# Long expert lists in a branch with two arms, a router that reads x itself, and later head norms

## The chip, the cores and the metric

One core of a Trainium2 chip. The metric is device time of one execution in microseconds (us), as the median of three runs. TensorE (PE) multiplies; its weight loads are listed apart as PEld. VectorE (DVE) and ScalarE (ACT) do elementwise work and empty the accumulators in PSUM, GpSimd (POOL) helps and issues some transfers, and SyncE (SP) issues most of them.

## The reference, cut to what matters

256 tokens of width 1024 in float32 pass four layers: two of a first block, two of a second. A layer of the first block is a token mixer and a mixture of 16 experts:

```
h = rmsnorm(x, norm2_g) * (1 + sc2) + sh2
scores = sigmoid(h @ w_router)              # 16 experts in 4 groups of 4
# best group by the sum of its two best (score + bias); its two best experts;
# their scores, normed to sum 1, are the weights in combine
for e in range(16):
    he = silu(h @ w_gate[e]) * (h @ w_up[e])      # 1024 -> 512
    y += combine[:, e] * (he @ w_down[e])         # 512 -> 1024
x = x + g2 * y
```

Each token so goes to 2 of 16 experts, and how many tokens an expert gets depends on the data. The second block begins with an attention in which 16 query heads and 4 key heads of width 64 are normed per head (rmsnorm over 64), turned by position, and scored against 256 own and 256 context keys, in a window and with a sink.

## The kernel before, in words

Everything is kept as xT: features on partitions (8 chunks of 128, KD), 256 tokens along the row. Wide products are done as three products of rounded operands: a weight is split into a high part (ScalarE, L513) and the rest (VectorE or POOL, L514), an activation likewise, and mm3 (L532 to L534) multiplies high by high, high by low and low by high. Products of plain float32 operands are two instructions each in the trace.

The program is written as straight Python, unrolled. A scheduler orders each engine's instructions by its own estimate of when they are ready, with program order as priority. An If is a unit for it: nothing moves over its borders, each engine takes the branch for itself, and a shorter path adds to the semaphores what the longer one would have.

**Token mixer, end (L986 to L993).** A loop of four turns multiplies by w_out, adds the result to two chunks of xT (L990) and squares them; when all eight are summed, rnorm, the reciprocal root of the mean square of each token, is made by Ln and Exp (L399, L400).

**Router (L1059 to L1129).** hf = norm of xT with gain and shift (eight VectorE or POOL products, eight ScalarE passes), the router's product with hf in four column groups of the array (L1067), a copy, two transposes and a sum into tokens by experts (L1075), the clamp (L1076), the sigmoid as Exp, Ln, Exp, and some 20 small VectorE steps to combine weights (cmb), and to each token's place in its experts' lists (pos). Beside it hf is turned into rows per token (L1137) and split into ht, high and low (L440, L441).

**Experts (L1340 to L1376).** A list has 64 places (SL). places makes a 0/1 table of tokens by places for four experts (PG), features multiplies ht by it, which gathers the tokens' columns (xg), in four steps of two chunks, each emptied by one copy (evac, VectorE and ScalarE in turn). For each expert e: gate_up, 64 places against 512 columns of gate and up (L1179, L1180); swiglu (Silu on ScalarE, product on VectorE); place(e - 2), which scatters expert e-2's weighted result into yT with its table PT (L1258); down of expert e-1 (L1224, L1225), whose result ScalarE and VectorE weight and split into y (L1228, L1229); turn, four transposes of the hidden row and a VectorE copy into he (L1203, L1204). After every even expert scatter_tab makes PT and the weights of two experts. After the third and fourth of a group of four, half of the next group's features. Last comes an If (L1373): a list longer than 64 runs beyond, which gathers the rest of the list, and does gate, up, down and scatter for up to 32 more places by themselves; a nested If (L1308) goes on with longer lists still.

**Weights.** An expert has six transfers of 1 MB. ahead(6e + 14) asks at expert e for what fills the queue to two experts ahead, on SP and POOL in turn; each waits for its buffer.

**Window attention (L1522 on).** For keys of context and own tokens, then for four groups of query heads: projection, head_norm (copy with gain, square, product with a swapping table, product that sums squares, turn by position, root, product), then copies into high and low parts. Then 16 units score (L1580 high key part over 128 rows, L1581 low key part over the 64 rows of the head's high query part), take softmax and multiply with values.

Of the kernel before, what the change touches and what calls it, by code (L numbers as in the profile page):

```python
# [18 lines left out]
T = 256  # L19
# [89 lines left out]
def tile_kernel(ctx, tc, A, out, dbg=None, stop=None):  # L109
# [97 lines left out]
    wrt = ctile([128, KD, 2 * NE], name="wrt")  # L207
    wnorm = ctile([128, 2], name="wnorm")

    def later_rows():  # L210
        nc.sync.dma_start(rbias, A["router_bias"][None, :].to_broadcast([128, NE]))
        nc.sync.dma_start(sink, A["win_sink_2"].to_broadcast([128, 16]))
        for j in range(2):
            nc.sync.dma_start(wrt[:, :, NE * j:NE * j + NE], A["w_router"].rearrange("(k p) e -> p k e", p=128))
# [350 lines left out]
    def token_mix(l):  # L565
        key = (0, l)
        with ExitStack() as es:
# [418 lines left out]
            st = Stats(P, lambda: sp.tile([128, T], F32, name=nm("sq"), tag="sq"))  # L986
            for n in range(4):
                ps = dense2(P, split_w(load_w(A["w_out"][l], 0, 8, 256 * n, 256), hlp, 8), mga, 8)
                for e in range(2):
                    V.scalar_tensor_tensor(xT[:, 2 * n + e], ps[:, e], mod(key, 2, 2 * n + e), xT[:, 2 * n + e], op0=OP.mult, op1=OP.add)  # L990
                    st.add(2 * n + e)
                ada(f"o{n}")
        dump(f"x_tm{l}", xT)  # L993
# [48 lines left out]
    def moe(l, experts):  # L1042
        key = (0, l)
        with ExitStack() as es:
# [14 lines left out]
            hf = mp.tile([128, KD, T], F32, name="hf", tag="b8", bufs=2)  # L1059
            gn = gain(key, 4, "norm2_g", 8 * l, f"gn2_{l}")  # L1060
            norm_split(xT, gn, lambda k: mod(key, 3, k), P, sp, [hf[:, k] for k in range(KD)], r=rnorm)
            dump(f"hf{l}", hf)

            lgp = ps_("gu")
            for k in range(KD):
                g = k % 4
                PE.matmul(lgp[32 * g:32 * g + 32, 0:T], wrt[:, k], hf[:, k], start=(k < 4), stop=(k >= 4), skip_group_check=True)  # L1067
            lgs = sp.tile([128, 512], F32, name=nm("lgs"), tag="gx", bufs=1)[:, 0:T]
            S.copy(lgs, lgp[:, 0:T])
            lgt = ps_("t")  # L1070
            for t in range(2):
                PE.transpose(lgt[:, 128 * t:128 * t + 128], lgs[:, 128 * t:128 * t + 128], ident)
            rt = mp.tile([128, 4, 2, NE], F32, name="rt")
            sc_, bi, cmb, pos = (rt[:, i] for i in range(4))
            V.tensor_reduce(sc_, lgt[:, 0:T].rearrange("p (t g e) -> p t e g", t=2, g=4)[:, :, 0:NE], axis=AX.X, op=OP.add)  # L1075
# [57 lines left out]
            for t in range(2):  # L1133
                for g in range(2):
                    ps = ps_("gu")
                    for k in range(4):
                        PE.transpose(ps[:, 128 * k:128 * k + 128], hf[:, 4 * g + k, 128 * t:128 * t + 128], ident)  # L1137
                    sl = slice(512 * g, 512 * g + 512)
                    split_act(ht[0][:, t, sl], ht[1][:, t, sl], ps)

            tc.keep_in_program_order(S.preload_act_table_set("silu_and_others"))

            def gather(dst, cols_, ks):

                for k0 in ks:
# [6 lines left out]
                    evac(dst[:, k0:k0 + 2], ps.rearrange("p (k n) -> p k n", n=T))  # L1152

            def scatter_tab(pg, es_, wc, tabs, tag="t"):

                m = len(es_)
                n = m * SL
                pw = sp.tile([128, 2, 2 * SL], F32, name=nm("pw"), tag="pw", bufs=1)
                ps = ps_(tag)
                for t in range(2):  # L1160
                    V.tensor_tensor(pw[:, t, :n].rearrange("p (e s) -> p e s", e=m), pg(t).bitcast(F32).rearrange("p (e s) -> p e s", e=m),
                                    cmb[:, t, es_[0]:es_[0] + m, None].to_broadcast([128, m, SL]), OP.mult)
                    PE.transpose(ps[:n, 128 * t:128 * t + 128], pw[:, t, :n], ident)
                j = sp.tile([128, T], BF, name=nm("jk"), tag="jk", bufs=1)
                S.activation(j[:n], ps[:n, :T], AF.Copy, accum_out=wc[:n])
                for i, (pt, w) in enumerate(tabs):
                    for r in (0, 64):
                        V.tensor_scalar(pt[r:r + 64], ps[SL * i:SL * i + SL, :T], 0.0, None, op0=OP.is_gt)
                        V.tensor_copy(w[r:r + 64], wc[SL * i:SL * i + SL])
# [49 lines left out]

            def down(he, e, w, y, tag):  # L1220

                py = ps_(tag)
                for j in range(4):
                    PE.matmul(py[0:64], he[:, j], cut(e, j, 0), start=(j == 0), stop=(j == 3), skip_group_check=True)  # L1224
                    m = PE.matmul(py[64:128], he[:, j], cut(e, j, 1), start=(j == 0), stop=(j == 3), skip_group_check=True)  # L1225
                    if j == 1:
                        yield m.ins
                S.activation(y[0], py, AF.Copy, scale=w)  # L1228
                V.scalar_tensor_tensor(y[1], py, w, y[0].bitcast(F32), op0=OP.mult, op1=OP.subtract)  # L1229
                yield m.ins  # L1230
# [29 lines left out]
            def beyond(e, w, level):  # L1260
# [12 lines left out]
                for h in range(2):  # L1273
                    ps = ps_("y" if h else "gu")
# [10 lines left out]
                evac(xo.rearrange("p (h j) s -> p j h s", h=2), ps.rearrange("p (j h s) -> p j h s", j=4, h=2))  # L1285
                ptl = sp.tile([128, T], F32R, name=nm("pto"), tag="pto", bufs=1)
                wc = sp.tile([128, 2], F32, name=nm("wc"), tag="wc", bufs=1)
                scatter_tab(lambda t: pg[:, t, 0:SL], [e], wc[:, 0:1], [(ptl, wc[:, 1:2])])
# [10 lines left out]
                y = [sp.tile([128, 512], F32R, name=nm("yo"), tag=f"yo{i}", bufs=1) for i in range(2)]  # L1299
# [5 lines left out]
                yield m  # L1305
# [6 lines left out]
            he_ = mp.tile([128, 4, SL], F32, name="he")  # L1312
# [28 lines left out]
            for e in range(NE):  # L1341
# [16 lines left out]
                place(e - 2)  # L1358
                if e:
                    for _ in down(he_, e - 1, tabs[e - 1][1], y_, "y"):  # L1360
                        pass
                turn(x_, he_)
                if e % 2 == 0:
                    for i in (e, e + 1):
                        tabs[i] = (mp.tile([128, T], F32R, name=nm("PT"), tag="PT", bufs=3),
                                   sp.tile([128, 1], F32, name=nm("w2"), tag="w2", bufs=3))
                    wc = sp.tile([128, 1], F32, name=nm("wp"), tag="wp")
                    scatter_tab(lambda t: lists[g][:, t, SL * j:SL * j + 2 * SL], [e, e + 1], wc, [tabs[e], tabs[e + 1]], "gu")
# [17 lines left out]
            if l:  # L1386
                mark = sp.tile([128, 1], F32, name=nm("mark"), tag="wp")
                with tc.issue_after(S.copy(mark, he_[:, 0, 0:1]).ins):
# [8 lines left out]
            for h in range(2):  # L1397
                fs = slice(256 * h, 256 * h + 256)
                py = ps_("t" if h else "y")[:, 0:256]
                for j in range(4):  # L1400
                    for q in range(2):
                        PE.matmul(py[64 * q:64 * q + 64], he_[:, j], cut(NE - 1, j, h)[:, 256 * q:256 * q + 256], start=(j == 0), stop=(j == 3),
# [25 lines left out]
    def win_attention(l, key):  # L1428
        with ExitStack() as es:
# [95 lines left out]
            def head_norm(ps, gcol, turn):  # L1525
# [4 lines left out]
                S.activation(s_, ps, AF.Square)  # L1530
                if turn:
# [11 lines left out]
                return x  # L1543


            for c, (a, th, tl) in ((1, (hc, ch, cl)), (0, (h, hh, hl))):
                ps = dense2(P, wk, a, 8)
# [263 lines left out]
```

## Time and profile before

| | |
|---|---|
| median of three runs | 1977.56 us (1974.22 to 1979.89) |
| the profiled execution | 1981.36 us, of which the profile's span is 1979.5 |
| instructions | 30922 |
| mean granted TensorE clock | 0.951 |
| data moved | 467.37 MB, 236 GB/s over the span |
| expert stages | 340.67 to some 640 us, and 949.93 to some 1240 us |

A stretch's busy time is the union of an engine's instructions in it. PEclk is the clock that the chip granted TensorE: 1.00 is 2.4 GHz, 0.50 is 1.2 GHz, a value in between a mean. An idle time in brackets stands ahead of an instruction, with what released it; a q behind an engine's name is its sequencer. 35 passes through swiglu in the trace are 32 experts and 3 long lists.

### The profile page before, as it was taken

What the parts mean: (1) busy time and instruction counts of PE and PEld (TensorE: products, weight loads), DVE (VectorE), ACT (ScalarE), POOL (GpSimd) and SP (SyncE); (2) the same over time, 40 slices, a digit from 0 to 9 for tenths busy, and PEclk for the clock granted to TensorE, in tenths of its full rate; (3) what the DMA queues carried; (4) which work ended last, traced back from release to release, by engine and by line L of the source; (5) the groups of instructions that cost most, each with busy time, mean ns of one, the idle gap of its engine ahead of it and who ended that gap; (6) DMA issues with size and microseconds to landing.
All of it is one profiled execution on the core that took longest, in us unless ns stands there. A gap on an engine that the chain in (4) does not pass through costs nothing. (4 is left out here: it accounts for less than half of the span.)

```text
span 1979.5 us, 30922 instructions
## 1 busy us (share of the span) xinstructions
PE 1779.8 (90%) x12451; PEld 1329.2 (67%) x12451; DVE 1034.1 (52%) x1893; ACT 885.6 (45%) x1492; POOL 323.1 (16%) x244
## 2 busy tenths in 40 slices
PE   6989998887888899998888977789899998989997
PEld 4767796334343777787434433666789997979997
DVE  5766454222122886555222222686466776677775
ACT  4544543111112544454111112886567675457874
POOL 2310241111111320233011110230200002430000
PEclk9999998998899899998899988899999999999998
DMA  9767784894896466896599955330386734576430
GB/s 324 256 231 293 275 285 188 339 384 174 300 412 241 170 220 239 297 337 222 224 403 407 391 219 193 118 128 1 124 300 236 264 130 171 181 259 210 171 106 22
DMA packets 264655, 467.37 MB, mean 236 GB/s; under 512 B 10322, under 2 KB 139328, under 8 KB 264432
## 3 DMA queue, kind: packets, MB, share of 16 engines
q1 hardware_dynamic: 240576, 374.74, 52.8%
q0 software_dynamic: 23200, 88.32, 11.4%
q8 instruction: 141, 2.31, 0.4%
q10 hardware_dynamic: 656, 1.32, 0.2%
q14 instruction: 82, 0.67, 0.1%
HBM read 463.31 MB, written 1.05 MB: 235 GB/s over the span
## 5 line engine op out<-in xcount | busy, mean ns | idle before, releaser
L532 PE MATMUL mm<-hh,hi 128*128 128x256 f32 x1584 | 460.3, 291 | 15.5 <-ACT hh L455 10.9
L534 PE MATMUL mm<-hh,lo 128*128 128x256 f32 x1584 | 458.0, 289 | 5.4 <-DVE lo L514 5.4
L533 PE MATMUL mm<-hl,hi 128*128 128x256 f32 x1584 | 456.1, 288 | 7.4 <-DVE hl L456 5.7
L513 ACT CAST hi<-w 128x1024 fp32r<-128x1024 f32 (+4 forms) x330 | 307.6, 970 | 168.6 <-PE mm L533 122.4
L532 PEld LDWEIGHTS mm<-hh,hi 128*128 128x128 f32 x1584 | 309.1, 195 | 29.6 <-ACT hh L455 13.8
L514 DVE TENSOR_TENSOR lo<-w,hi 128x1024 fp32r<-128x1024 f32 (+4 forms) x260 | 293.4, 1145 | 68.0 <-ACT hi L513 67.7
L534 PEld LDWEIGHTS mm<-hh,lo 128*128 128x128 f32 x1584 | 308.6, 195 | 10.6 <-DVE lo L514 6.8
L533 PEld LDWEIGHTS mm<-hl,hi 128*128 128x128 f32 x1584 | 309.0, 195 | 9.7 <-DVE hl L456 6.6
L514 POOL TENSOR_TENSOR lo<-w,hi 128x1024 fp32r<-128x1024 f32 x70 | 174.9, 2502 | 827.4 <-ACT hi L513 757.6
L1179 PE MATMUL ps<-w,xg 128*64 128x512 f32 x512 | 249.3, 644 | 32.8 <-DVEq L1373 32.8
L1180 PE MATMUL ps<-w,xg 128*64 128x512 f32 x512 | 249.9, 645 | 1.1 <-issue 1.1
L1179 PEld LDWEIGHTS ps<-w,xg 128*64 128x64 f32 x512 | 72.9, 148 | 172.4 <-issue 171.9
L1197 DVE TENSOR_TENSOR gx<-gx,ps 64x512 f32<-64x512 f32 (+1 forms) x35 | 23.4, 669 | 279.1 <-ACT gx L1196 279.1
L1196 ACT ACTIVATE gx<-ps 64x512 f32<-64x512 f32 (+1 forms) x35 | 20.0, 573 | 330.3 <-PE ps L1180 318.5
L1224 PE MATMUL ps<-w,he 128*64 128x512 f32 x240 | 109.3, 598 | 0.0
L1225 PE MATMUL ps<-w,he 128*64 128x512 f32 x240 | 109.3, 598 | 0.0
L367 PE MATMUL ps<-w,crep 128*32 128x512 f32 x768 | 106.0, 605 | 3.0 <-DMA w<-in_ada_w_dram 1.5
L532 PE MATMUL yT<-zh,hi 128*128 128x256 f32 x352 | 100.6, 286 | 4.2 <-ACT zh L440 4.2
L533 PE MATMUL yT<-zl,hi 128*128 128x256 f32 x352 | 100.8, 286 | 1.1 <-DVE zl L441 1.0
L534 PE MATMUL yT<-zh,lo 128*128 128x256 f32 x352 | 100.2, 285 | 0.0
L532 PE MATMUL mm<-half,hi 128*128 128x256 f32 x320 | 93.3, 292 | 2.3 <-ACT half L440 2.3
L533 PE MATMUL mm<-half,hi 128*128 128x256 f32 x320 | 92.8, 290 | 0.7 <-DVE half L441 0.7
(469 smaller groups left out, 3206.3 us busy)
## 6 DMA issues: line engine op xcount, KB each, us to landing
w<-in_ada_w_dram SPq DMA_DIRECT2D x96, 1024.0 KB, 7.0
w<-in_w_up_dram SPq DMA_DIRECT2D x64, 1024.0 KB, 13.4
w<-in_w_gate_dram POOLq DMA_DIRECT2D x56, 1024.0 KB, 10.8
w<-in_ffn_w_up_dram SPq DMA_DIRECT2D x44, 1024.0 KB, 5.0
w<-in_w_in_dram SPq DMA_DIRECT2D x36, 1024.0 KB, 10.2
w<-in_w_down_dram SPq DMA_DIRECT2D x36, 1024.0 KB, 10.4
w<-in_w_down_dram POOLq DMA_DIRECT2D x28, 1024.0 KB, 9.9
w<-in_ffn_w_down_dram SPq DMA_DIRECT2D x22, 1024.0 KB, 6.7
```

What stands on the lines that cost most here:

```text
L367: PE.matmul(ps[32 * g:32 * g + 32], crep[blk][:, 4 * s + g, SLOTS - 1 - i:SLOTS + 31 - i], w[i][s][:, g], start=(i + s == 0), stop=(i == n ...
L513: S.copy(hi, raw)
L514: (lo_eng or V).tensor_tensor(lo, raw, hi.bitcast(F32), OP.subtract)
L532: PE.matmul(ps, wh, ah, start=start, stop=False, skip_group_check=True)
L533: PE.matmul(ps, wh, al, start=False, stop=False, skip_group_check=True)
L534: latest[0] = PE.matmul(ps, wl, ah, start=False, stop=stop, skip_group_check=True).ins
L1179: PE.matmul(ps[0:64], xg[:, k, off:off + SL], wg[k // 4][:, k % 4], start=(k == 0), stop=(k == KD - 1), skip_group_check=True)
L1180: m = PE.matmul(ps[64:128], xg[:, k, off:off + SL], wu[k // 4][:, k % 4], start=(k == 0), stop=(k == KD - 1), skip_group_check=True)
L1196: S.activation(x_, ps[0:64], AF.Silu)
L1197: V.tensor_tensor(x_, x_, ps[64:128], OP.mult)
L1224: PE.matmul(py[0:64], he[:, j], cut(e, j, 0), start=(j == 0), stop=(j == 3), skip_group_check=True)
L1225: m = PE.matmul(py[64:128], he[:, j], cut(e, j, 1), start=(j == 0), stop=(j == 3), skip_group_check=True)
```

## The change

1. **The branch.** The If moves from the end of an expert to the place behind swiglu and the expert's table, and gets a second arm. Long arm: the gather of beyond, place, its transposes and table, turn, half of the down products, its gate and up, the other half, and the rest of beyond. Short arm: place, turn, all down products. The weighting of the down result stands behind both arms. he has two buffers. beyond uses y instead of tiles of its own.
2. **Tables per expert**, each written at once for all 128 partitions.
3. **The router reads xT.** Gain times router weights (wrg) is made before the w_out loop, as is shift times router weights (logit0). Each w_out turn multiplies its two new chunks of xT by wrg. In moe the sum is scaled per token by rnorm, which is turned into a column by a one-row product (rtok). There is no hf: xT itself is transposed, ht is scaled by rtok, and gain and shift are applied to the gathered columns as they leave PSUM (gained).
4. **Attention.** The low key score takes all 128 rows (low by low is added), each head_norm's rest is issued behind the next projection, and all query weights are split by ScalarE and VectorE.

The diff, cut to its core:

```diff
@@ end of token_mix
+            lg = P.tile([128, 2, T], F32, name=nm("lg"), tag="o")[:, 0]
+            V.tensor_tensor(wrg, wrt, experts.gn[:, :, None].to_broadcast([128, KD, NE]), OP.mult)
+            for k in range(KD):
+                PE.matmul(lg[:, 64:64 + NE], mod(key, 3, k).to_broadcast([128, 128]), wrt[:, k], start=(k == 0), stop=(k == KD - 1), skip_group_check=True)
+            S.copy(logit0, lg[:, 64:64 + NE])
             for n in range(4):
                 ps = dense2(...)
                 for e in range(2):
...
+                    for t in range(2):
+                        PE.matmul(lg[:, NE * t:NE * t + NE], xT[:, k, 128 * t:128 * t + 128], wrg[:, k], start=False, stop=(k == KD - 1), skip_group_check=True)
+            S.copy(lgs, lg[:, 0:2 * NE].rearrange("p (t e) -> p t e", t=2))
@@ moe
-            norm_split(xT, gn, lambda k: mod(key, 3, k), P, sp, [hf[:, k] for k in range(KD)], r=rnorm)
...
+            for k in range(KD):
+                for t in range(2):
+                    PE.transpose(xps[:, t, 128 * k:128 * k + 128], xT[:, k, 128 * t:128 * t + 128], ident)
+            for t in range(2):
+                PE.matmul(rps[:, t:t + 1], rnorm[0:1, 128 * t:128 * t + 128], ones[0:1, 0:1], start=(t == 0), stop=True, skip_group_check=True)
+            V.tensor_copy(rtok, rps[:, 0:2])
+            for t in range(2):
+                V.scalar_tensor_tensor(sc_[:, t], lgs[:, t], rtok[:, t:t + 1], logit0, op0=OP.mult, op1=OP.add)
...
+                    S.activation(ht[0][:, t, sl], xps[:, t, sl], AF.Copy, scale=rtok[:, t:t + 1])
+                    V.scalar_tensor_tensor(ht[1][:, t, sl], xps[:, t, sl], rtok[:, t:t + 1], ht[0][:, t, sl].bitcast(F32), op0=OP.mult, op1=OP.subtract)
...
+            def gained(dst, ps, k0, n):
+                for i in range(n):
+                    k = k0 + i
+                    if i % 2:
+                        S.activation(dst[:, k], ps[:, i], AF.Identity, scale=gn[:, k:k + 1], bias=mod(key, 3, k))
+                    else:
+                        V.tensor_scalar(dst[:, k], ps[:, i], gn[:, k:k + 1], mod(key, 3, k), op0=OP.mult, op1=OP.add)
@@ the loop over experts, behind swiglu
-                place(e - 2)
-                if e:
-                    for _ in down(he_, e - 1, tabs[e - 1][1], y_, "y"):
-                        pass
-                turn(x_, he_)
-                if e % 2 == 0:
...
-                    scatter_tab(lambda t: lists[g][:, t, SL * j:SL * j + 2 * SL], [e, e + 1], wc, [tabs[e], tabs[e + 1]], "gu")
+                scatter_tab(lambda t: lists[g][:, t, SL * j:SL * j + SL], e, *tabs[e])
+                py = ps_("y") if e else None
+                with tc.If(counts[j] > SL, label=f"over{l}_{e}") as longer:
+                    more = beyond(e, w, 1)
+                    next(more)
+                    place(e - 2)
+                    next(more)
+                    turn(x_, he[e])
+                    second((0, 1))
+                    next(more)
+                    second((2, 3))
+                    run(more)
+                with longer.Else():
+                    place(e - 2)
+                    turn(x_, he[e])
+                    second(range(4))
+                if e:
+                    weighted(py, tabs[e - 1][1], y_)
                 if g < 3 and j >= 2:
                     if j == 2:
                         places(g + 1)
                     features(g + 1, range(4 * j - 8, 4 * j - 4, 2))
-                with tc.If(counts[j] > SL, label=f"over{l}_{e}"):
-                    for _ in beyond(e, w, 1):
-                        pass
@@ window attention
-                    PE.matmul(sc[e], qe[pe], kl[pe, kv].rearrange("p a b -> p (a b)"), start=False, stop=False, skip_group_check=True)
+                    PE.matmul(sc[e], qe, kl[:, kv].rearrange("p a b -> p (a b)"), start=False, stop=False, skip_group_check=True)
...
+            for i in range(4):
+                q = queries(i, w)
+                next(q)
+                if i < 3:
+                    w = wq(i + 1)
+                if behind:
+                    next(behind)
+                behind = q
+            next(behind)
```

second(js) is the down products of expert e-1 for the row quarters js. queries and the like for keys run a projection and the first two steps of head_norm up to their first stop, and the rest at the second.

## Rows read from the trace of the kernel before

**Rows 1.** The page, part 1: busy time of each engine, share of span.
```profile
PE 1779.8 (90%) x12451; PEld 1329.2 (67%) x12451; DVE 1034.1 (52%) x1893; ACT 885.6 (45%) x1492; POOL 323.1 (16%) x244
```
**Rows 2.** Stretches: length, busy time per engine (instructions), PEclk, DMA share, GB/s.
```profile
340.67:611.95 271.28, 232.18 (x1343) 103.25 (x1343) 63.43 (x171) 32.66 (x67) 34.71 (x49) 0.95 0.83 317
949.93:1208.35 258.42, 223.79 (x1216) 98.70 (x1215) 58.43 (x153) 29.25 (x59) 31.02 (x43) 0.93 0.86 332
1023.89:1039.34 15.45, 14.28 (x69) 5.74 (x69) 1.96 (x4) 1.28 (x2) 1.92 (x3) 0.89 1.00 387
1039.34:1055.83 16.49, 15.12 (x87) 7.42 (x88) 5.64 (x16) 2.35 (x5) 1.73 (x3) 1.00 1.03 404
...
430.88:465.80 34.92, 27.61 (x216) 14.54 (x216) 10.63 (x34) 5.76 (x13) 6.27 (x10) 0.93 0.59 228
465.80:501.44 35.64, 29.01 (x213) 14.40 (x213) 7.96 (x24) 5.29 (x11) 5.86 (x10) 0.88 0.49 178
1151.18:1190.28 39.10, 29.02 (x197) 13.43 (x197) 7.27 (x23) 4.70 (x10) 3.52 (x6) 0.81 0.35 140
297.00:320.90 23.90, 22.87 (x165) 21.23 (x164) 11.80 (x15) 7.87 (x14) 6.43 (x4) 0.93 0.41 149
320.90:340.67 19.77, 13.02 (x73) 8.50 (x72) 11.14 (x41) 9.39 (x20) 3.16 (x5) 0.83 0.73 288
```
**Rows 3.** Waits, all engines: who waited for whom, us, times, longest.
```profile
PE ps L1179 <- DVEq L1373: 32.8, 25, 2.7
```
**Rows 4.** PE in order of time, 1022 to 1057 us: start, us, line, shape.
```profile
1023.88 0.69 PE L1179 MATMUL ps<-w,xg 128*64 128x512 f32 x1 [2.53 <-DVEq L1373]
...
1032.60 1.21 PE L1258 MATMUL ps<-PT,y 64*128 64x256 f32 x15
1033.74 0.64 PE L1224 MATMUL ps<-w,he 128*64 128x512 f32 x1
...
1037.32 0.46 PE L1203 MATMUL ps<-cst,gx 64*128 64x64 f32 x4
1038.23 0.38 PE L1258 MATMUL ps<-PT,y 64*128 64x256 f32 x1 [0.45 <-ACTq L1373]
1039.34 0.61 PE L1179 MATMUL ps<-w,xg 128*64 128x512 f32 x1 [0.72 <-DVEq L1373]
...
1053.54 1.22 PE L1150 MATMUL ps<-PG,ht 128*128 128x256 f32 x8 [0.68 <-ACTq L1373]
```
**Rows 5.** DVE in order of time, in the same stretch.
```profile
1023.08 0.43 DVE L1168 TENSOR_SCALAR PT<-ps 64x256 fp32r<-64x256 f32 x1
...
1038.28 0.75 DVE L1229 SCALAR_TENSOR_TENSOR y<-ps,w,y 128x512 fp32r<-128x512 f32 x1
```
**Rows 6.** DMA issues, 1025 to 1125 us: count, size, median us to landing.
```profile
w<-in_w_up_dram SPq DMA_DIRECT2D x12, 1024.0 KB, 15.7
```
**Rows 7.** PE in order of time, the long list of layer 1.
```profile
1166.67 2.92 PE L1277 MATMUL ps<-ht,pg 128*128 128x512 f32 x8 [1.91 <-DVE pg L1271]
...
1189.77 0.57 PE L1258 MATMUL ps<-PT,y 64*128 64x256 f32 x1 [3.46 <-PEq L1308]
```
**Rows 8.** ACT in order of time, end of the root, layer 0.
```profile
320.49 0.42 ACT L400 ACTIVATE rnorm<-rnorm 128x256 f32<-128x256 f32 x1
```
**Rows 9.** DVE in order of time: the clamp and the lists, layer 0.
```profile
329.45 0.17 DVE L1076 TENSOR_SCALAR rt<-rt 128x32 f32<-128x32 f32 x1
...
334.71 0.75 DVE L1330 TENSOR_TENSOR PG<-cst,rt 128x256 fp32r<-128x256 f32 x2
```
**Rows 10.** Groups by line: shapes, count, busy us, mean ns, idle before.
```profile
L771 PE MATMUL o<-half,half 128*128 128x64 f32 x32 | 5.3, 248 | 0.0
...
L1580 PE MATMUL mm<-kh,cl 128*128 128x512 f32 x16 | 7.8, 489 | 1.0 <-ACT pw L1588 1.0
L1581 PE MATMUL mm<-kl,cl 64*128 64x512 f32 x16 | 7.9, 497 | 0.0
L1533 PE MATMUL ps<-xk,cst 128*128 128x512 f32 x10 | 6.3, 719 | 5.8 <-ACT xk L1528 5.8
```

More of the change, by code (lines that the diff above doesn't have):

```diff
@@ L1218, in cut, with down_mm, weighted @@
                 return wd[h][:, j] if e == NE - 1 else wd[j // 2][:, j % 2, 512 * h:512 * h + 512]
+            def down_mm(py, he, e, js):
+                for j in js:
+                    PE.matmul(py[0:64], he[:, j], cut(e, j, 0), start=(j == 0), stop=(j == 3), skip_group_check=True)
+                    m = PE.matmul(py[64:128], he[:, j], cut(e, j, 1), start=(j == 0), stop=(j == 3), skip_group_check=True)
+                return m.ins
+            def weighted(py, w, y):
+                S.activation(y[0], py, AF.Copy, scale=w)
+                V.scalar_tensor_tensor(y[1], py, w, y[0].bitcast(F32), op0=OP.mult, op1=OP.subtract)
             def down(he, e, w, y, tag):
                 py = ps_(tag)
[L1223 to L1230, printed above, removed]
+                m = down_mm(py, he, e, range(4))
+                weighted(py, w, y)
+                yield m
             def down_few(he, e, w, y, tag):
@@ L1298, in beyond @@
                 (turn_few if level == 1 else turn)(x_, he)
-                y = [sp.tile([128, 512], F32R, name=nm("yo"), tag=f"yo{i}", bufs=1) for i in range(2)]
+                y = y_
                 if level == 1:
@@ L1304, in beyond @@
                     pass
-                yield m
                 scatter(y, ptl)
@@ L1387, in moe @@
                 mark = sp.tile([128, 1], F32, name=nm("mark"), tag="wp")
-                with tc.issue_after(S.copy(mark, he_[:, 0, 0:1]).ins):
+                with tc.issue_after(S.copy(mark, he[NE - 1][:, 0, 0:1]).ins):
                     exp_ln_tables()
@@ L1542, in head_norm, with keys @@
                 V.tensor_tensor(x, x, s_, OP.mult)
-                return x
-            for c, (a, th, tl) in ((1, (hc, ch, cl)), (0, (h, hh, hl))):
-                ps = dense2(P, wk, a, 8)
-                x_ = head_norm(ps, wnorm[:, 1:2], c == 0)
+                yield x
+            qs = [x.rearrange("p (a b) t -> p a b t", b=2) for x in (ch, cl)]
+            def keys(c, a):
+                x = head_norm(dense2(P, wk, a, 8), wnorm[:, 1:2], c == 0)
+                next(x)
+                yield
+                x_ = next(x)
                 for p in range(2):
@@ L1554, in win_attention, with queries, wq @@
                         V.tensor_tensor(kl[64 * d:64 * d + 64, p:4:2, c], x_[ph], kh[ph, p:4:2, c].bitcast(F32), OP.subtract)
[L1555 to L1567 removed]
+                yield
+            def queries(i, w):
+                g, s = divmod(i, 2)
+                x = head_norm(dense2(P, w, h, 8), wnorm[:, 0:1], True)
+                next(x)
+                yield
+                x_ = next(x)
+                for p in range(2):
+                    ph, pl = slice(64 * p, 64 * p + 64), slice(64 - 64 * p, 128 - 64 * p)
+                    hi = qs[g][ph, 2 * s:2 * s + 2, p]
+                    S.copy(hi, x_[ph])
+                    V.tensor_tensor(qs[g][pl, 2 * s:2 * s + 2, p], x_[ph], hi.bitcast(F32), OP.subtract)
+                yield
+            def wq(i):
+                return split_w(load_w(w_qkv, 0, 8, 256 * i, 256), hlp, 8, engs=(V, V))
+            k1 = keys(1, hc)
+            next(k1)
+            evac(vt[:, 2:4], dense_tok(P, wv, ch, cl))
+            next(k1)
+            k0 = keys(0, h)
+            next(k0)
+            w = wq(0)
+            evac(vt[:, 0:2], dense_tok(P, wv, hh, hl))
+            next(k0)
+            ada_fill("win.k", P, sp)
+            behind = None
+            for i in range(4):
[7 more added lines that the diff above has]
+            next(behind)
             scale = 0.125
```

92 lines of the change are left out of this document (35 added, 57 removed).

## The prediction

> **What bounds the kernel now.** I read the busy shares first: TensorE works through nine tenths of the span and no other engine through much over half [rows 1], so a change pays where TensorE stands still, or where it runs at the lower of its two clocks. Then the table by stretches, put around the places of the diff [rows 2]. The two expert stages last 271.28 and 258.42 us, with TensorE busy for 232.18 and 223.79, so it idles 39.1 and 34.6 us there. The three experts with long lists hold 7.3, 6.6 and 10.1 us of that (34.92 - 27.61, 35.64 - 29.01, 39.10 - 29.02). What is left is 25.2 us in one layer and 24.5 in the other, over 13 and 14 experts. The granted clock of the stages is 0.95 and 0.93. A level of half speed for a tenth of the time gives a mean of 0.95, so 27 and 36 us ran at 1.2 GHz, and up to 13.6 and 18.1 us were lost by it.
>
> Third, the list of waits: the largest of TensorE in the program is the first product of an expert waiting for VectorE at the line of the If, 25 times, 32.8 us [rows 3]. Fourth, one expert in order of time [rows 4, 5]. Products with gate and up start at 1023.88, the earlier expert's scatter at 1032.60, the down products at 1033.74, the turn of the hidden row at 1037.32, and by 1037.78 nothing is left. The next expert starts at 1039.34. In between stand 0.45 and 0.72 us of idle time: VectorE has its subtraction of 0.75 us (1038.28) in front of the If, and the first product behind the If waits until VectorE has passed it. After an even expert VectorE also has the tables of two experts there (the last at 1023.08) and TensorE stands for 2.53 us; the stretch behind that runs at a clock of 0.89 where the next one has 1.00 [rows 2].
>
> **Part 1, the If in the middle of the expert.** In the new order place, turn and the down products lie in both arms, and the join stands behind them. VectorE's last work in the short arm is the copy behind the turn, some 3.5 us (the length of the down products, 1033.74 to 1037.32 in rows 4) before TensorE reaches the join, and the subtraction and the tables lie before or behind the arms. So the two gaps and the 2.53 us should go. Late next is the pipe emptying at the join: the smallest step of that kind in the rows is the 0.45 us at 1038.23, and I take it for each expert, which leaves 13 x 0.45 = 5.9 and 14 x 0.45 = 6.3 of the 25.2 and 24.5 us. At the entry of the arm place (1.21 us) covers most of Silu and the product with up before the turn can start. The If itself costs nothing more as long as TensorE's sequencer is ahead of its array, since the jump is taken while products are queued; if that cover goes, rival 3 has the price. The clock returns perhaps 2 us a layer, from the 1.7 us that the stretch with 0.89 lost (15.45 x 0.11) and the few like it.
>
> Tables per expert: two more transposes and one ScalarE pass for each second expert, and fewer, longer VectorE operations. The transposes lie on TensorE; four small ones take 0.46 us (1037.32), so seven or eight times 0.23 us is 1.7 us a layer. VectorE and ScalarE do their share while gate and up run (they stand for most of those 7 us), so nothing. The gathered rows now get gain and shift as they are taken from PSUM, by two engines half each: no more elements than now; the 0.68 us before the second gather (1053.54) may go, bounds 0 and -4 us in all. Sum: 25.2 - 5.9 + 2 - 1.7 = 19.6 and 24.5 - 6.3 + 2 - 1.7 = 18.5, so **-38 us**, bounds 0 (the waits change places) and -60 (all idle time and some clock).
>
> Is there another limit under it? The weights. An expert has six transfers of 1.049 MB, and the stretches run at 387 to 404 GB/s [rows 2], with the slowest kind landing 15.7 us after issue [rows 6]. At 404 GB/s six need 15.6 us; an expert now takes 15.45 to 16.49 and would take some 14.3. The code asks for the gate and up of expert e+2 at expert e, so nearly two experts (31 us) less 15.7 us to landing leaves 15 us in hand. Each fast expert eats 1.3, twelve of them (layer 1 before its long list) 15.6: just covered.
>
> The Trainium skill ("DMA: Bandwidth & Descriptors", Specifications) puts the HBM limit of one core at about 358 GB/s. By it six transfers would need 17.6 us (an estimate from that page), more than an expert takes now, and this part would gain nothing. The trace disagrees, with 404 GB/s over a whole expert.
>
> **Part 2, long lists in the arm.** Three experts. Their own gather, transposes and few-column products run between place, turn and the two halves of the down products. Before, TensorE waited at each step (1.91 us for the list at 1166.67, 3.46 at the scatter behind the nested If at 1189.77 [rows 7]). Of 24.0 us idle the steps up to the hidden row are now covered by other products, those of the last scatter are not; about half goes, and the eight small VectorE operations for gain and shift lie under the turn and the first half of down. **-13 us**, bounds 0 and -24.
>
> **Part 3, router on x.** From the end of the reciprocal root (320.91 [rows 8]) to the clamp of the scores (329.45 [rows 9]) are 8.5 us of norm, products, copy, transposes and reduction, with TensorE idle for a third of the stretch [rows 2]. In their place: two one-row products, a small copy and two small VectorE operations, each like the 0.17 us at 329.45 plus a hand-over; an estimate is 1.5 us, so -7.0. The four subtractions for the token rows, two of which lie before the clamp's chain today or in its gaps, now start with that chain and push the lists (334.71) back by one, 0.7 us: -6.3 a layer, bounds -8 and -3. The turning of x and the products that set yT to zero have TensorE's idle time as cover.
>
> It is not free: 24 small products a layer move into the w_out loop, where TensorE is busy 22.87 of 23.90 us [rows 2]. Each is two instructions with a 128-column weight load; the nearest group is 5.3 us for 32 [rows 10], 0.17 us each with twice or four times the columns. I take 0.11, so 48 x 0.11 = 5.3 us, of which the last 1.0 us falls in idle time: +4.3, bounds 0 and +8. Gain, weights and SP's one load less are off the path. Both layers: **-4 us** (bounds -16 and +10).
>
> **Part 4, attention.** The low score with 64 rows takes 497 ns and the high one with 128 rows 489 [rows 10]: 128 rows cost nothing, bounds -1 and +1. The norms finish behind the next projection's products; TensorE waited 5.8 us for them in all [rows 10]. The low parts of half of the query weights move from POOL to VectorE, which had slack there. **-3 us**, bounds -6 and +5.
>
> **Sum.** -38 - 13 - 4 - 3 = -58 us. The profiled execution took 1981.36 us (span 1979.5), 3.8 above the median of the runs, so it would take 1923; against the median of 1977.56 the forecast is **1920 us**, with its own range 1895 to 1945. A measurement of this kernel tells 0.3%, some 6 us, from no change.
>
> **Rivals.** *1. The join waits as the If did.* If the turn comes last in the short arm, behind the down products, VectorE's copy and its step to the join again follow TensorE's last product. For it: the down products don't need Silu and are ready earlier than the turn. Against it: place covers about as long as Silu takes. Price: 0.45 + 0.72 us for 27 experts, 32 us of the 38 are not gained: 1952. Chance 0.20. *2. Weights bound the stage.* If what is in hand is eaten early (the last two transfers of an expert are asked for late), experts settle at 15.6 us. Against 15.45 to 16.49 now, 23 of them gain some 0.6 each, with the first two of a layer 8 more: 22 instead of 38, so 1936. For it: DMA shares of 1.00 and more [rows 2]; against it: not one wait for weights among the experts' waits. Chance 0.14. *3. Slower: the jump into the second arm.* Every expert now jumps over a long arm of code to reach the short one, with the join's empty pipe behind. For it: at 1189.77 TensorE stood 3.46 us on its own sequencer after a nested If [rows 7]. Against it: at the ordinary Ifs nothing like it stands [rows 4]. At 3.46 us for each of 32 experts it is +111, so 1920 + 111 = 2031; it decides from 58 / 32 = 1.8 us per expert. Chance 0.07.
>
> The Trainium skill ("Runtime: NRT & Kernel Launch", Instruction fetch mechanics) says that a taken branch whose target lies outside the fetched pages stalls for the fetch. That is rival 3's mechanism; the jumps over the old If's body were such branches too, and of 25 waits there the longest is 2.7 us [rows 3].
>
> *4. The change does nothing measurable:* the arms keep their waits and the products in w_out eat the router's gain: about 1975. Chance 0.04.
>
> **How the numbers follow.** Forecast 0.55, rivals 0.20, 0.14, 0.07 and 0.04. The range of 8 in 10 goes from the forecast with the experts and long lists at their far bounds (22 and some 10 us more: 1888) to rival 1 with the router at its costly bound (1952 + 10: 1962), and holds rival 2. Faster by over 0.3%: the forecast and rivals 1 and 2 are 0.89; less a little of rival 1's tail, 0.88. Within 0.3%: 0.05. Slower: 0.07.
>
> **What would show it.** Right: the wait of the gate product for VectorE at the If is gone, an expert takes 13 to 15 us, the three long ones 29 to 33, and from reciprocal root to the first expert product 13 us instead of 20. Wrong: waits of the same size at the join for VectorE or for TensorE's own sequencer, waits for w, w_out loops longer by over 8 us, or the expert stages still over 250 us.

## The result and the profile after

The changed kernel takes 1906.7 us (median; 1905.0 to 1913.1), the one before 1977.7: a ratio of 0.9649 [0.9622, 0.9676]. The forecast was 1920, its own range 1895 to 1945. The sum was 58 us and came out as 69 to 71, but two effects larger than that difference stood in no term. First the rows that answer to those of before. Busy times [rows 1]:

```profile
PE 1739.3 (91%) x12551; PEld 1314.8 (69%) x12551; DVE 1032.4 (54%) x1858; ACT 801.7 (42%) x1454; POOL 315.9 (17%) x236
```

ScalarE lost 83.9 us of busy time with only 38 instructions fewer. Nothing in the diff removes as much work.

The stretches [rows 2]: both expert stages; an ordinary expert; the third and fourth of a group of four, with a gather; the three long lists; w_out loop, here from its first addition to xT (the row of before begins 2.1 us ahead of it); root to first expert product; two stretches of layer 1's experts:

```profile
341.51:597.35 255.84, 228.87 (x1355) 100.66 (x1356) 61.94 (x152) 37.13 (x83) 34.73 (x49) 0.97 0.87 328
931.51:1181.28 249.77, 215.37 (x1226) 90.48 (x1228) 54.85 (x129) 34.13 (x76) 30.98 (x43) 0.97 0.90 339
410.98:423.82 12.84, 12.39 (x74) 4.89 (x72) 2.78 (x6) 1.75 (x4) 2.21 (x4) 1.00 1.03 388
518.80:536.13 17.33, 15.09 (x92) 6.94 (x88) 5.66 (x12) 3.37 (x8) 3.21 (x5) 1.00 1.03 393
536.13:551.57 15.44, 14.36 (x86) 6.59 (x86) 3.36 (x8) 2.48 (x5) 2.21 (x3) 1.00 1.03 393
423.82:459.85 36.03, 30.77 (x220) 15.75 (x216) 12.31 (x35) 6.32 (x15) 6.84 (x11) 0.91 0.71 263
459.85:493.06 33.21, 28.41 (x214) 14.61 (x214) 9.70 (x30) 5.25 (x11) 5.88 (x9) 0.95 0.49 179
1133.15:1165.90 32.75, 25.72 (x202) 11.70 (x198) 10.23 (x30) 5.28 (x12) 3.58 (x6) 0.94 0.54 197
298.46:322.46 24.00, 22.99 (x184) 22.33 (x183) 11.79 (x15) 7.37 (x15) 6.45 (x4) 0.99 0.43 148
322.46:341.51 19.05, 12.17 (x65) 10.06 (x63) 9.66 (x40) 6.78 (x13) 1.56 (x3) 0.65 0.79 300
...
1000.00:1040.00 40.00, 36.95 (x218) 15.68 (x215) 9.90 (x22) 6.27 (x14) 5.27 (x8) 1.00 1.03 392
1040.00:1080.00 40.00, 35.24 (x188) 13.63 (x184) 7.45 (x16) 5.28 (x11) 6.66 (x9) 1.00 1.03 392
```

The stages shortened by 15.4 and 8.7 us, not by the 51 of the forecast. An ordinary expert takes 12.84 us with 0.45 us idle; one with a gather takes 17.3 or 15.4, no less than the 16.49 and 15.35 of before. With the DMA share at 1.03 the rate is 392 GB/s, where the forecast counted on 404.

TensorE's waits in both stages [rows 3]:

```profile
PE ps L1215 <- DVE PT L1181: 10.1, 18, 1.6
PE ps L1191 <- ACT xg L1157: 7.0, 12, 0.7
PE ps L1192 <- DMA w<-in_w_up_dram: 7.0, 3, 3.2
PE ps L1168 <- DVE PG L1348: 6.4, 5, 1.3
...
PE ps L1234 <- DMA w<-in_w_down_dram: 4.2, 4, 2.4
...
PE ps L1275 <- issue: 3.9, 3, 1.5
...
PE ps L1191 <- issue: 2.9, 1, 2.9
```

The 32.8 us at the If are gone, as forecast, and nothing of the kind waits at the join. At the entry of the second arm the scatter (L1275) stood three times for nothing that the profile shows (issue), 3.9 us in all; the one gate product that did so, for 2.9 us at 1165.88, follows layer 1's long arm. New are waits for weights, 11.2 us in all, and for the gather's evacuation. One expert in order of time [rows 4]:

```profile
417.93 0.44 PE L1178 MATMUL ps<-cst,pw 128*128 128x128 f32 x2
418.29 1.22 PE L1275 MATMUL ps<-PT,y 64*128 64x256 f32 x16
419.96 0.43 PE L1215 MATMUL ps<-cst,gx 64*128 64x64 f32 x4 [0.45 <-DVE PT L1181]
420.32 0.64 PE L1234 MATMUL ps<-w,he 128*64 128x512 f32 x1
...
423.38 0.59 PE L1235 MATMUL ps<-w,he 128*64 128x512 f32 x1
423.80 0.59 PE L1191 MATMUL ps<-w,xg 128*64 128x512 f32 x1
```

Scatter, turn and down run through the arm, and the next expert's gate product (423.80) begins before the last down product ends. The one gap, 0.45 us, is the size that the forecast left for each expert, though at another place. Last, ScalarE's table loads, before and then after:

```profile
L244 ACT ACT_TABLE_LOAD x22 | 28.2, 1283 | 0.4
L245 ACT ACT_TABLE_LOAD x22 | 28.2, 1283 | 0.4
L399 ACT ACT_TABLE_LOAD x12 | 15.4, 1283 | 0.2
L400 ACT ACT_TABLE_LOAD x12 | 15.4, 1283 | 0.2
L257 ACT ACT_TABLE_LOAD x4 | 5.1, 1283 | 4.7 <-DMA stage<-in_c_dram 4.6
L1141 ACT ACT_TABLE_LOAD x2 | 2.6, 1283 | 0.0
L314 ACT ACT_TABLE_LOAD x1 | 1.3, 1283 | 0.0
L1394 ACT ACT_TABLE_LOAD x1 | 1.3, 1283 | 0.0
```

```profile
L259 ACT ACT_TABLE_LOAD x4 | 5.1, 1283 | 4.7 <-DMA stage<-in_c_dram 4.6
L1151 ACT ACT_TABLE_LOAD x2 | 2.6, 1283 | 0.0
L316 ACT ACT_TABLE_LOAD x1 | 1.3, 1283 | 0.0
```

76 loads became 7. The 69 that went are 88.5 us of ScalarE: more than all of its missing busy time. Here is where they began, ScalarE behind layer 1's last expert, before:

```profile
1222.74 0.19 ACT L1388 COPY mark<-he 128x1 f32<-128x1 f32 x1
1222.95 1.28 ACT L257 ACT_TABLE_LOAD   x1
1224.24 1.28 ACT L1394 ACT_TABLE_LOAD   x1
...
1227.74 1.28 ACT L399 ACT_TABLE_LOAD   x1
1229.03 0.48 ACT L399 ACTIVATE rs<-rs,epsc 128x1 f32<-128x1 f32 x2
1229.53 1.28 ACT L400 ACT_TABLE_LOAD   x1
```

The common table of Exp and Ln (L257) is tied to mark, a copy of the last hidden row. Before, that row was written in front of the last If, so the load stood there too; a long list's arm runs Silu, and behind the join the next function brings its own load, then Ln and Exp one each, to the program's end. In the changed kernel the hidden row is written in both arms, so mark and its load moved behind the join, and every Ln and Exp after it shares them. The Trainium skill ("ScalarE activation tables: per-element evaluation and per-set limits", Table sets in the compiler and the runtime) says that the back end places table loads per block; the rows agree with it, since the load before a join counted for nothing behind it.

### The profile page after: what moved, and what is told of

Its sections match the earlier page's. It is cut to its first block, busy times and chain, and to the rows that moved or that the text cites. A ratio compares the mean times of both kernels' runs of the same rounds, so it can differ in the third digit from the quotient of the medians.

```text
span 1906.1 us, 31042 instructions
## 1 busy us (share of the span) xinstructions
PE 1739.3 (91%) x12551; PEld 1314.8 (69%) x12551; DVE 1032.4 (54%) x1858; ACT 801.7 (42%) x1454; POOL 315.9 (17%) x236
## 5 line engine op out<-in xcount | busy, mean ns | idle before, releaser
L516 DVE TENSOR_TENSOR lo<-w,hi 128x1024 fp32r<-128x1024 f32 (+4 forms) x264 | 302.1, 1157 | 94.7 <-ACT hi L515 94.4
L516 POOL TENSOR_TENSOR lo<-w,hi 128x1024 fp32r<-128x1024 f32 x66 | 167.8, 2547 | 799.3 <-ACT hi L515 799.3
L1191 PE MATMUL ps<-w,xg 128*64 128x512 f32 x512 | 232.0, 606 | 11.4 <-ACT xg L1157 7.0
L1192 PE MATMUL ps<-w,xg 128*64 128x512 f32 x512 | 232.2, 607 | 7.0 <-DMA w<-in_w_up_dram 7.0
L1209 DVE TENSOR_TENSOR gx<-gx,ps 64x512 f32<-64x512 f32 (+1 forms) x35 | 23.4, 669 | 237.4 <-ACT gx L1208 191.4
L1234 PE MATMUL ps<-w,he 128*64 128x512 f32 x240 | 113.1, 608 | 4.2 <-DMA w<-in_w_down_dram 4.2
L1235 PE MATMUL ps<-w,he 128*64 128x512 f32 x240 | 112.4, 606 | 0.1
```

Of the source, the lines that this page charges most:

```text
L516: (lo_eng or V).tensor_tensor(lo, raw, hi.bitcast(F32), OP.subtract)
L1191: PE.matmul(ps[0:64], xg[:, k, off:off + SL], wg[k // 4][:, k % 4], start=(k == 0), stop=(k == KD - 1), skip_group_check=True)
L1192: m = PE.matmul(ps[64:128], xg[:, k, off:off + SL], wu[k // 4][:, k % 4], start=(k == 0), stop=(k == KD - 1), skip_group_check=True)
L1209: V.tensor_tensor(x_, x_, ps[64:128], OP.mult)
```

## The experiments

Theory T: beside the forecast's parts the kernel gained by the table loads, and the router's part cost time. Rival A: the forecast's terms hold, and what attention and ffn gained is clock and order.

**1. The kernel before, its load kept.**

```
-                with tc.issue_after(S.copy(mark, he_[:, 0, 0:1]).ins):
+                with tc.issue_after(S.copy(mark, yT[:, 0, 0:1]).ins):
```

> The kernel before with one change: the load of ScalarE's combined exp and ln table is tied to an instruction behind the last expert's If instead of one in front of it. Theory T (a side effect of the change, which the forecast had no term for): before, the load stood in front of the join, was lost there, and 69 loads of 1.28 us each followed in layer 1's tail, attention and both ffn stages; after, none of them is there. Then this kernel has 7 loads in all, and takes 1943 us (34 us less: some 12 in attention, 18 in the two ffn stages, 4 in the tail), with the expert stages unchanged at 271 and 258 us. Rival A (attention and ffn gained through the new order of attention and through a higher granted clock; the loads lie beside TensorE's work): 1972 to 1978 us.

1949.3 us, ratio 0.9859 [0.9832, 0.9886]: 28 us less (22 to 33) by one moved load. It has the 7 loads of the changed kernel, and two waits of VectorE for ScalarE, at L1631 and L1722, fell from 62.5 and 32.3 us to 43.0 and 6.3. T holds, at 28 instead of 34.

**2. Experts undone** (the loop, tables and long arm of before, in the changed kernel).

```
-                with tc.If(counts[j] > SL, ...) as longer:
-                    ...
-                with longer.Else():
-                    ...
+                with tc.If(counts[j] > SL, ...):      # last in the expert
+                    for _ in beyond(e, w, 1): pass
```

> The changed kernel with the experts' part undone (If at the end, tables for two experts together, long lists in one piece behind the If); router and attention stay changed, and the exp and ln table load stays behind the join. Theory T: the experts' part is worth what the two stages shortened by in the traces, 15.4 and 8.7 us: 1906.7 + 24 = 1931 us. Rival A (the experts' part is worth the forecast's 51 us, part of it in the stages behind): 1958 us.

1958.8 us, 0.9920 [0.9897, 0.9944]: 54 us slower than the changed kernel, where T had 24; A's number is met. But this is not the experts' part alone: behind the old order, gain and shift at the gather cost more (the third and fourth expert of a group take 18.0 to 18.2 and 17.3 to 18.6 us here, 16.5 and 15.3 in the kernel before; some 22 us over the ten without long lists).

**3. Attention undone** (its three edits).

```
-                    PE.matmul(sc[e], qe, kl[:, kv]...)
+                    PE.matmul(sc[e], qe[pe], kl[pe, kv]...)
-                yield        # head norm behind the next projection
-    split_w(..., engs=(V, V))
+    split_w(...)
```

> The changed kernel with attention's part undone (64-row low scores, each head norm right behind its projection, low halves of the query weights as before). Theory T: this part is worth the forecast's 3 us (bounds -5 and +6), the rest of what attention gained belongs to the table loads: 1907 to 1912 us. Rival A (the new order of attention gave the 15 us by which that stage shortened): 1920 to 1925 us.

1919.2 us, 0.9718 [0.9698, 0.9737]: 14 us slower (7 to 20). T's 3 us are wrong, and A was nearly right here.

**4. Router undone** (normed copy, products and transposes of before; gathered rows emptied by a plain copy).

```
-                    gained(dst, ps.rearrange("p (k n) -> p k n", n=T), k0, 2)
+                    evac(dst[:, k0:k0 + 2], ps.rearrange("p (k n) -> p k n", n=T))
```

> The changed kernel with the router's part undone (a normed copy of x, its products and its transposes, no small products in the w_out loop, gathered rows without gain and shift). From the traces: each w_out loop 2.2 us shorter, the way from root to first expert product 0.7 and 4.4 us longer: 1906 to 1908 us, no difference that can be measured. The forecast's own terms (4 us for both layers): 1911 us. If gain and shift at the gather cost time (the experts with a gather take 17.3 and 15.4 us, against 16.5 and 15.3 before): up to 8 us less, 1899 us.

1888.9 us, 0.9561 [0.9534, 0.9588]: 17 us faster than the changed kernel, more than any theory had. In the trace the third and fourth expert take 16.78 and 14.58 us where no weights are late (ten such experts without long lists, 7 us if each gains as much), waits for weights are 2.2 us instead of 11.2, and the rate is 407 to 414 GB/s. What else differed that could touch a transfer was a start address: the router's tiles lie in front of all weight buffers, and hold 1216 bytes of each partition instead of 1024. The first buffer starts at byte 38656 in the old layout (256 beyond a multiple of 512) and at 38848 in the new (448 beyond); the others follow by 8192 bytes each, so all have that remainder. Theory S: that sets the rate.

**5. Start moved by 64 bytes.** An unused tile behind the constants of the changed kernel.

```
     wnorm = ctile([128, 2], name="wnorm")
+    ctile([128, 16], name="pad")
```

> The changed kernel with 64 unused bytes more behind its constants and nothing else. Theory S: the new router's small tiles (192 bytes more of constants) moved all weight buffers from a start of 256 to one of 448 beyond a multiple of 512 bytes; the saturated DMA then moves 391 to 394 GB/s (the kernels with the new router) instead of 407 to 414 (those with the old one), and experts wait for weights. With the buffers at a multiple of 512 the rate is 407 to 414 again, TensorE's 11.2 us of waits for weights are nearly gone, and the time is 8 to 11 us less: 1896 to 1899 us. Rival B (the rate is lower because of something else in the new router, or the waits come from the faster experts alone): rate 391 to 394, time unchanged at 1907 us.

1890.6 us, 0.9559 [0.9537, 0.9581]: 18 us less (11 to 25) by 64 unused bytes. The two stretches that show 392 GB/s after:

```profile
1000.00:1040.00 40.00, 36.67 (x208) 16.00 (x206) 9.02 (x19) 6.28 (x13) 6.63 (x9) 1.00 1.03 412
1040.00:1080.00 40.00, 34.05 (x188) 13.05 (x184) 8.00 (x18) 4.56 (x11) 6.65 (x9) 0.96 1.03 414
```

Waits for weights fell to 4.5 us. S holds; its price was set too low. The waits are not all of it: behind the longest of the changed kernel, 3.16 us at 572.07, the granted clock was 0.50 up to 578 us, and the gate products came every 0.85 us instead of every 0.43.

**6. The kernel before, moved by 192 bytes** (`ctile([128, 48], name="pad")` at the same place).

> The kernel before with 192 unused bytes more behind its constants and nothing else, so that its weight buffers start where those of the changed kernel do. Theory S: the saturated rate falls from 395 to 411 GB/s to 391 to 394; an expert's six transfers then need 16.0 us against the 15.4 to 16.5 that it takes, so the expert stages grow a little: 1980 to 1990 us. Rival B: rate and time unchanged, 1976 us.

1976.6 us, 0.9993 [0.9978, 1.0009]. The stretches of before, and then those of this kernel:

```profile
978.00:1018.00 40.00, 37.97 (x219) 18.12 (x217) 8.22 (x19) 4.80 (x9) 4.44 (x6) 1.00 1.03 408
1058.00:1098.00 40.00, 36.52 (x195) 15.96 (x193) 7.40 (x18) 4.21 (x8) 4.45 (x6) 0.91 1.03 411
```

```profile
978.00:1018.00 40.00, 37.72 (x218) 17.37 (x215) 8.23 (x19) 4.79 (x9) 5.19 (x7) 1.00 1.03 391
1058.00:1098.00 40.00, 36.53 (x195) 16.00 (x193) 7.54 (x18) 4.21 (x8) 4.45 (x6) 0.91 1.03 393
```

The rate fell as S says, the time did not, and neither kernel has a wait for an expert's weights: at the old pace the buffers in hand covered it. The address costs only once the experts are faster.

**7. Long list in one piece.**

```
-                    (place, turn and down woven between the steps of beyond)
+                    place(e - 2); turn(x_, he[e]); second(range(4))
+                    run(beyond(e, w, 1))
```

> The changed kernel with the long list's work in one piece behind place, turn and the down products of its arm, not woven between them (the arms and the tables per expert stay). If the weaving is worth the forecast's 13 us: 1920 us. From the traces, where the three long experts cost 56.4 us over an ordinary one at their place after and 64.0 before: 1914 us. If only the place of the If counts: 1907 us.

1901.2 us, 0.9613 [0.9592, 0.9634], below all three and 7 us less than the changed kernel (0 to 14). The long experts take 99.9 us in all, 102.0 in the changed kernel. Weaving gains nothing that these runs can tell.

**8. Next lists ahead of the weighted rows** (on the kernel of experiment 4; `places(g + 1)` moved in front of `weighted`).

> The changed kernel with the old router (as in the run with the old router, 1889 us) and the next four lists built ahead of the weighted rows on VectorE. There the gather of the third expert of each four waits 8.4 us in all, six times, for VectorE's second list, which stands behind the weighted rows. If that wait is the path: 1881 to 1883 us. If weights or the second gather's evacuation come next: 1887 to 1889 us.

1888.6 us, 0.9535 [0.9505, 0.9565], as experiment 4. The third experts fell from 16.78 to 15.21 us, but the stages did not shorten (249.1 and 237.4 us; 246.6 and 236.2 in experiment 4): others waited for weights, 5.8 us instead of 2.2.

**9. The low scores alone as before** (the 64 rows of experiment 3, norms and splits kept).

> The changed kernel with the low scores alone as before (64 rows instead of 128); the later head norms and VectorE's splits stay. The forecast priced the 128 rows at nothing (bounds -1 and +1): 1907 us, and then the 13 to 14 us by which undoing all of attention's part slowed the kernel belong to the norms. Theory R: in the trace with attention's part undone the score loop repeats in 20.6 us for each five steps where the changed kernel needs 18.5, so the rows carry some 6.6 us: 1911 to 1916 us, with the repeat back at 20.6 us.

1915.9 us, 0.9679 [0.9661, 0.9698]: 6 us slower, an interval of -1 to +12; the score loop repeats in 20.6 us instead of 18.5. In three repeats that is 6.3 us. So the rows carry about 6, and norms with splits the remaining 7 or 8. Its score products by line, and then those of the changed kernel [rows 10]:

```profile
L1638 PE MATMUL mm<-kh,cl 128*128 128x512 f32 x16 | 7.8, 488 | 0.5 <-ACT pw L1646 0.5
L1639 PE MATMUL mm<-kl,cl 64*128 64x512 f32 x16 | 8.0, 497 | 0.0
```

```profile
L1638 PE MATMUL mm<-kh,cl 128*128 128x512 f32 x16 | 7.5, 472 | 0.5 <-ACT pw L1646 0.5
L1639 PE MATMUL mm<-kl,cl 128*128 128x512 f32 x16 | 6.7, 419 | 0.0
```

**10. Old router, moved by 192 bytes** (experiment 4 with the tile of 6).

> The changed kernel with the old router and 192 unused bytes behind its constants: the old router with its weight buffers where the changed kernel has them. Theory S (the 17 us that the router's part costs are the buffers' start): the saturated rate is 391 to 394 GB/s, waits for weights come back, and the time is that of the changed kernel, 1902 to 1909 us. Rival B (they are the new router's own work, products in the w_out loop and gain at the gather): 1889 us.

1905.2 us, 0.9629 [0.9608, 0.9651]: 13 us slower than experiment 4 (7 to 20), at 392 to 393 GB/s. The same stretch of layer 1 in experiment 4, and then here:

```profile
1030.00:1070.00 40.00, 37.72 (x214) 15.87 (x214) 8.40 (x17) 5.85 (x13) 5.51 (x8) 1.00 1.03 414
```

```profile
1030.00:1070.00 40.00, 37.28 (x212) 15.45 (x210) 7.75 (x17) 4.68 (x10) 4.42 (x6) 1.00 1.03 393
```

With 4, 5 and the changed kernel the square is complete: good start 1889 (old router) and 1891 (new), bad start 1905 and 1907. The router itself is worth nothing that these runs can tell.

**11 and 12. Fewer bytes**, on the changed kernel and on experiment 8. The second halves of gate and up are left out from the second expert of each layer on; the long lists stay at the same three experts.

```
+                    if not j and e and i > 1:
+                        ...                            # 32 KB into the buffer, unused
+                        w = self.wts[e, 0][i - 2]
```

> The changed kernel with two of an expert's six weight transfers left out from the second expert of each layer on (the second halves of gate and up are computed with the first halves again); the products are as many and as large as before. Theory S: waits for weights are all that the buffers' start costs; without them an expert takes 12.9, 12.9, 17.3 or 15.4 us throughout, layer 0's stage is 4.6 and layer 1's 16 us shorter than in the changed kernel: 1884 to 1888 us. Rival (the engines bound the stages): 1900 to 1907 us.

1885.6 us, 0.9536 [0.9515, 0.9557]. Stages of 248.9 and 235.1 us, no wait for weights, ordinary experts 12.84 to 12.97 (without the first of a layer and the one ahead of layer 1's long list), as where weights are in time in experiment 5. So the address works through late weights, by the waits and the clock behind them.

> The kernel with the old router and the lists built ahead of the weighted rows, with the same two of six transfers left out from the second expert of each layer on. If the 9 us that the earlier lists take out of six experts were eaten by waits for weights: periods of 12.9, 12.9, 15.2 and 14.6 us throughout, some 5 and 12 us less in the stages, 1870 to 1874 us. If something else ate them: 1885 to 1889 us.

1870.1 us, 0.9457 [0.9438, 0.9476], stages of 243.6 and 227.0. So 15 us of experiment 8 (8 to 22) are weights that are late even at 410 GB/s. They are not all that is left: without them TensorE still idles for 34 us of these stages. Experiments 4, 5 and 8, some 1889 to 1891 us, beat both kernels and can't be told from one another.

## Why the prediction was right, and where it was not

The runs give this account, against before (1976 us). The first term is the rest; it holds if the parts add, which experiment 2 shows they do only roughly:

| part | forecast | measured | from |
|---|---|---|---|
| If in two arms, tables per expert | -38 | -32 to -37 | rest |
| long lists in the arm, woven | -13 | -8, of it weaving 0 | the stretches; 7 |
| router's own work | -4 | about 0 | 4 against 5, 10 against after |
| router: start of the buffers | none | +13 to +18 | 5, 10 |
| attention | -3 | -14 | 3, 9 |
| table loads | none | -28 | 1 |

With the router of before (experiment 4) the two stages went from 529.7 to 482.7 us: 47 less, where the first two terms have 51.

**The sign and the main mechanism were right.** The wait at the If is gone, the turn does not come last in the arm, ordinary experts take 12.84 us (13 to 15 forecast), and behind the 29 jumps into the second arm no gate product stood for the branch; the scatter at the arm's entry has the 3.9 us above, not 3.46 for each. So rivals 1 and 3 fell. The prediction's "at the ordinary Ifs nothing like it stands" was read from one stretch; the list of waits of before has 19 on TensorE's sequencer at the If:

```profile
PE ps L1258 <- PEq L1373: 7.9, 19, 1.3
```

At that size they decide nothing. The gain lies in the first two experts of each four, 2.6 to 2.9 us each, not in all.

**Rival 2 came true in part.** "At 404 GB/s six need 15.6 us ... just covered": at 392 they need 16.0, and layer 1's experts from the eighth to the thirteenth take 16.0, 16.1, 14.0, 25.1, 16.3 and 15.7. Waits for w, and a stage over 250 us (255.8; the other 249.8), were signs that the prediction had named as wrong; without late weights the stages take 248.9 and 235.1 (experiment 11). The term failed by a resource taken as constant, the rate, which the change itself lowered, and by "just covered": even at 407 to 414 GB/s some weights came late (experiments 5 and 8).

**Router.** The w_out loop grew by 2.2 us a layer (4.3 forecast): from the first addition to xT (299.13 before) to the end of the root (320.91) it took 21.8 us, now 24.0. From root to first expert product 0.7 and 4.4 us went (6.3 each). TensorE in layer 0, in the place of [rows 8, 9]:

```profile
322.06 3.63 PE L1077 MATMUL ps<-cst,xT 128*128 128x128 f32 x16 [0.44 <-ACT rnorm L401]
325.61 0.60 PE L1083 MATMUL ps<-ones,rnorm 1*128 1x1 f32 x4
...
333.33 1.86 PE L1186 MATMUL ps<-chunkb 64*128 64x512 bf16 x4 [1.87 <-DVE ht L1149]
335.12 3.78 PE L1168 MATMUL ps<-PG,ht 128*128 128x256 f32 x16
```

The forecast gave transposes and zero products "TensorE's idle time as cover". They stand in front of what the chain waits for: the root ends at 322.46, but the one-row products come at 325.61, behind 16 transposes at the lower clock (granted 0.52; 3.63 us, and 1.94 in layer 1 at a clock of 1.00), and four zero products precede the gather. And "no more elements than now" for gain and shift was the wrong measure: the two experts of a group that gather became 0.56 and 0.86 us longer than with a plain copy, since the first gate product waits for ScalarE's last pass.

**Long lists.** The forecast let half of 24 us idle go; 7 went, and 17 are left. The three still take 36.0, 33.2 and 32.8 us (29 to 33 forecast), 102.0 together against 109.7 before. In one piece they take no more, so the cover by products woven between is what failed; what came is the arm's.

**Attention.** The prediction compared 497 with 489 ns in one trace and concluded that 128 rows cost nothing. Both rows came from a loop that mixes the two sizes. All at 128 rows they take 419 and 472 ns: the 64 rows between the 128 were a cost to both, some 6 us with an interval that holds 0, and the bounds of -1 and +1 were too near. The later norms with the splits gave 7 or 8 where 3 were forecast.

**Table loads.** No step failed here: one was missing. The diff shows he written in the arms; the trace of before had 69 loads in lines that the diff does not touch. ScalarE's own idle time says little of them, 0.2 to 0.4 us in front of each of their four lines; the 28 us come through ScalarE being late for the others, as VectorE's waits in experiment 1 show.

So the total came out in part by luck: two gains that the forecast lacked or had too small (28 and 11 us) covered a cost that it lacked (13 to 18) and two gains that did not come in full (5 of the long lists, 4 of the router).

## What to carry to other kernels

Read what a diff moves over a branch, not only what it edits: a state set ahead of a join (here a function table) can be lost behind it, and rows of the same load repeating down the program show it. Count the bytes that a change adds in front of DMA buffers, and keep their start where it was. Before crediting a stage with idle time, ask at what rate its transfers must then run, and leave a margin.

## What the hardware showed

**A buffer's start sets the rate.** With the DMA share at 1.03, starts of 256 and 0 beyond a multiple of 512 bytes gave 406 to 414 GB/s over 40 us stretches of layer 1, a start of 448 gave 391 to 394, in four kernels each. At a share of 1.01 or 1.02 the good starts too had stretches of 387 to 401. The Trainium skill ("DMA: Bandwidth & Descriptors", How a descriptor splits into AXI transactions) says that a piece that doesn't begin on 256 bytes has a first transaction from the boundary below, whose bytes ahead of the start are fetched and not used. It speaks of bytes fetched, while here the side written is off the boundary; by the same rule rows of 2 and 4 KB would take some 8% longer (an estimate from that page of the Trainium skill), and 4 to 5% were measured. Starts between were not tried.

**Mixed row counts cost both sides.** A 64-row product between 128-row ones takes 497 ns, the same product with 128 rows among its like 419; the 128-row products beside it take 488 and 472. Products of 64 rows among their like were not run.

**A table load is 1283 ns** in every row, and the next function follows some 0.01 us behind it (1227.74 to 1229.03). The Trainium skill ("ScalarE: Activation LUTs", What ACT_TABLE_LOAD costs) has the same 1283 ns and a drain of about 1380 ns more; no row here shows that drain.
